# A conditioned decoder trunk on one core: sum and copy of each feed-forward unit joined on VectorE, and one recurrent weight group's low part planned 200 positions ahead

## The chip, the cores and the metric

The kernel runs on one core of a Trainium2 chip. Five engines of that core work side by side, each through its own list of instructions in a fixed order: TensorE (PE in the profile; PEld is its weight load), VectorE (DVE), ScalarE (ACT), GpSimd (POOL) and SyncE (SP), which starts nearly all DMA transfers. They wait for each other by semaphores. An instruction that has to wait holds up everything behind it on its own engine.

The metric is the device time of one execution in microseconds. Before the change it is 1255.91 us, the median of three executions (1254.83 to 1256.75).

## The reference

One inference step of a two-layer decoder for a prompt (1 sequence of 512 tokens) and a batch of samples (8 sequences of 8 tokens), with D_MODEL 1024 and a feed-forward width D_FF of 2816, all in float32:

```python
for l in range(DEPTH):                                   # DEPTH = 2
    sh1, sc1, g1, sh2, sc2, g2 = ada_mod(c, ada_w[l], ada_b[l], 6)
    h = modulate(rms_norm(x, norm_g[l, 0]), sh1, sc1)
    if l < N_A_LAYERS:                                   # layer 0
        out, nbuf, h_last = recurrent_block(h, ...)
    else:                                                # layer 1
        q = apply_partial_rope(...(h @ attn_w_q[j])..., pos)
        out = sliding_sink_attention(q, k_all, v_all, sinks, p0) @ attn_w_o[j]
    x = x + g1[:, None, :] * out
    h = modulate(rms_norm(x, norm_g[l, 1]), sh2, sc2)
    x = x + g2[:, None, :] * swiglu(h, ffn_w_in[l], ffn_w_out[l])

def recurrent_block(h, ...):
    xr, yg = jnp.split(h @ w_in, 2, axis=-1)
    xr, new_buf = causal_dwconv(xr, conv_buf, conv_w, conv_b)
    o, h_last = rg_lru(xr, gate_w, gate_b, lam, h0)      # h = a*h + u, step by step
    return (o * jax.nn.gelu(yg, approximate=True)) @ w_out, new_buf, h_last

def swiglu(h, w_in, w_out):
    gate, up = jnp.split(h @ w_in, 2, axis=-1)
    return (jax.nn.silu(gate) * up) @ w_out
```

`ada_mod` is silu(c) times a weight matrix of 1024 x 6144, for each layer. Between the layers one key/value projection is made.

## The kernel before

**Tokens and precision.** The 576 tokens are kept as two halves h=0 and h=1 of 288 columns (256 of the prompt, 32 of samples). Activations lie as 128 channels by 288 columns. Every float32 operand of a product is split into a high part (rounded to the type that TensorE reads) and a low part (what is left); a product of one 128x128 weight block with one activation block is three matmuls: high weight by high activation, high weight by low activation, low weight by high activation.

**Weights.** They come by DMA in groups ("units") into four raw tiles. For each unit ScalarE casts the high part (tile names `wh`) and VectorE then subtracts it from the raw tile for the low part (also `wh`); this is `convert()` (L1036). The raw tile is free for the next DMA once the low part is made. Units 0 to 17 belong to the recurrent layer's input and gate weights; unit 18 is the first group of the recurrent output weight, whose tiles are raw25, wh49 (high) and wh50 (low). The conditioning weights (`ada_w`) come into five tiles `reg`; from each of them TensorE makes short matmuls with a stationary block `cz` (shown as `ada<-reg,cz`).

**Recurrent layer.** For each channel block VectorE, GpSimd and ScalarE make the gates, the products and a scan along the columns (`TENSOR_TENSOR_SCAN` in the profile); the scan's result, multiplied by the gelu of the other branch (tiles `ta69` to `ta72`), is split into a high and a low part (tiles `sl`; sl79 and sl80 are such a pair). `mm89` is the first block of the output projection: 24 matmuls over eight channel blocks, with wh49 and wh50 as weights, the first five of which are scanned well before.

**Feed-forward.** There are 22 units of 128 hidden channels per layer. For all but the first three, `seven()` (L1383) makes the two inner products (gate and up) for both token halves by a seven-product scheme of 2x2 blocks in place of eight: products "11", "12", "S1", "S2", "S3", "22", "S4" of 12 matmuls each. "S2", "S3" and "22" accumulate in one PSUM tile, bank "b": after S2, VectorE adds a copy of product "11" (`p1`, a `ta` tile) in place, then copies the sum out to `u2` (a `td` tile); S3 accumulates on the same tile and so its first matmul waits for both the sum and the copy. S4 goes to another bank, "e". This happens in 38 units, 19 for each layer. In the profile the sum reads `TENSOR_TENSOR mm<-mm,ta` and the copy `COPY td<-mm`; the matmuls of S2 use `h`, `tb`, `ta` and `sl` tiles by the unit, and those of S3 begin with `tb`.

**What sets the order.** The program is written once in a plain order and recorded: every instruction becomes an `Op` (L133 to L227) with a priority, its place in that order plus a bias. `schedule()` (L229) then plays the five engines through a table of estimated durations; on each engine it takes, among the ops that are ready or will be soon, by priority and time, and gives out the PSUM banks and buffers as they come free. The order that it finds is what each engine runs. `early(n)` (L578) lowers the priority number of what is written in it by n, so that it is planned as if it stood n positions further ahead. `together()` (L148) makes one `Op` of several instructions, which then stand directly behind each other. `HALVES` (L41) holds, by unit number, into how many pieces a low part is cut and how many positions ahead its cast and its low part are planned; units that are not in it have (1, 0). Since the planner goes by sums of durations, a change at one place can alter its choices at others.

All instructions are issued by one line, L491, so the profile's groups have to be told apart by tiles and operations.

Of the kernel before, what the change touches and what calls it, by code (L numbers as in the profile page):

```python
# [16 lines left out]
ALU = mybir.AluOpType  # L17
# [10 lines left out]
HC = 288  # L28
# [9 lines left out]
SWW = 2500.0  # L38
BETA = 0.75
ST = (1, 1, 1)  # L40
HALVES = {101: (2, 0), 103: (2, 60), 108: (1, 60)}  # L41
EW = EP = EA = EK = E1 = ER = 0
EN = 30
ES = 150
# [473 lines left out]
def trunk_kernel(ctx, tc, a):  # L518
    nc = tc.nc
    rec = Recorder(a["shadow"])  # L520
    V, S, G, T, Q = (Engine(rec, n, o) for n, o in (("DVE", nc.vector), ("ACT", nc.scalar), ("POOL", nc.gpsimd), ("PE", nc.tensor), ("SP", nc.sync)))
# [10 lines left out]
    def ps(pool=pmm, tag="mm"):  # L532
        cnt[0] += 1
        return rec.tile(pool, tag, NMM if tag == "mm" else (8 - NMM), RMM if tag == "mm" else 1, [P, 512], F32, f"{tag}{cnt[0]}")
# [12 lines left out]
    td = Slots(rec, cp, "td", SLOT, NTD)  # L547
# [29 lines left out]
    @contextmanager  # L577
    def early(n):  # L578

        rec.bias -= n  # L580
        yield
        rec.bias += n
# [453 lines left out]
    def convert():  # L1036
# [4 lines left out]
        u.hi, u.lo = whs(), whs()  # L1041
        parts, ahead_ = HALVES.get(nconv[0], (1, EW))
        with early(ahead_):
# [57 lines left out]
    def residual(h, o, c, g, last):  # L1101
        xp, xs = x[h][:, c, 0:HP], v48(x[h][:, c, HP:HC])
        V.scalar_tensor_tensor(xp, o[:, 0:HP], mp(g, c), xp, ALU.mult, ALU.add)
        t = ta()
        V.tensor_tensor(v48(t.f[:, 0:32]), v48(o[:, HP:HC]), msam(g, c, h), ALU.mult)
        (V if c >= KC - 2 else G).tensor_tensor(xs, xs, v48(t.f[:, 0:32]), ALU.add)
        t.done()
        if last and (g != L1 + G2 or c < KC - 1):
            square(h, c)
# [148 lines left out]
    for m in range(KC):  # L1258
# [3 lines left out]
            lambda h, o, m=m: residual(h, o, m, G1, True),  # L1262
# [8 lines left out]
    def ffn(l, g, after):  # L1271
# [95 lines left out]
        def pump(want=lambda: True):  # L1367
            while todo and (whs.live + todo[0][0] <= 2 * NHI):
                todo.popleft()[1]()
            assert want()  # L1370
            load_more()

        def right(name):

            if name in ("T2", "T3", "T4"):
                return [(p.r[:, 0:HC], q.r[:, 0:HC]) for p, q in X2[int(name[1])]]
            h, c0 = {"B11": (0, 0), "B21": (0, 4), "T1": (1, 0), "B22": (1, 4)}[name]
            v = h4r(h)
            return [(v[:, k, 0, :], v[:, k, 1, :]) for k in range(c0, c0 + 4)]
# [3 lines left out]
        def seven(i, name):  # L1383

            pump(lambda: (i, name) in W)
            w = W.pop((i, name))
            bank, ops = {"11": ("a", "B11"), "12": ("a", "B21"), "S1": ("e", "T1"), "S2": ("b", "T2"), "S3": ("b", "T3"),
                         "22": ("b", "T4"), "S4": ("e", "B22")}[name]
            b = B.setdefault(i, {})
            if bank not in b:  # L1390
                b[bank] = ps()
            o = b[bank][:, 0:HC]
            first = name in ("11", "S1", "S2")
            for k, (xh, xl) in enumerate(right(ops)):
                hi, lo = [w.r[:, q + k * P : q + (k + 1) * P] for q in (0, H2)]
                T.matmul(o, hi, xh, start=first and k == 0, stop=False, skip_group_check=True)
                T.matmul(o, hi, xl, start=False, stop=False, skip_group_check=True)
                T.matmul(o, lo, xh, start=False, stop=k == 3, skip_group_check=True)
            w.done()
            pump()  # L1400
            if name == "11":
                b["p1"] = ta()
                S.copy(b["p1"].f[:, 0:HC], o)
            elif name == "S1":
                b["p5"] = td()
                S.copy(b["p5"].f[:, 0:HC], o)
            elif name == "S2":

                V.tensor_tensor(o, o, b["p1"].f[:, 0:HC], ALU.add)
                b["p1"].done()  # L1410
                b["u2"] = td()
                V.tensor_copy(b["u2"].f[:, 0:HC], o)
            elif name == "12":

                b["g"] = ta()
                S.activation(b["g"].f[:, 0:HC], o, AF.Silu)
            elif name == "S3":

                y = b["p5"].f[:, 0:HC]
                V.tensor_tensor(y, o, y, ALU.add)  # L1420
            elif name == "22":

                y = b["g"].f[:, 0:HC]
                V.tensor_tensor(y, y, o, ALU.mult)
                whole(0, i, b["g"])
                del B[i]
            else:

                y, z = b["u2"].f[:, 0:HC], b["p5"].f[:, 0:HC]
                V.tensor_tensor(y, o, y, ALU.add)  # L1430
                S.activation(y, y, AF.Silu)
                G.tensor_tensor(z, y, z, ALU.mult)
                b["u2"].done()
                whole(1, i, b["p5"])

        def whole(h, f, t):
            m = mid[h][f] = (sl(F32R), sl(F32R))
            split(m[0].r[:, 0:HC], m[1].r[:, 0:HC], t.f[:, 0:HC])
            t.done()
# [20 lines left out]
        def emit():  # L1460
# [4 lines left out]
            for k in range(len(GROUPS)):  # L1465
                if k == 1 and l == 0:
                    sink_setup()
                for i in range(max(PLAIN, n_), n_ + GROUPS[k]):

                    if i == PLAIN:  # L1470
                        for j, w in ((0, "11"), (1, "11"), (0, "12")):
                            seven(i + j, w)
                    seven(i, "S1")
                    seven(i, "S2")
                    if i == PLAIN:
                        seven(i + 1, "12")
                    elif i > PLAIN + 1:
                        seven(i, "12")
                    if i > PLAIN and i + 1 < n_ + GROUPS[k]:
                        seven(i + 1, "11")  # L1480
                    seven(i, "S3")
                    ada_pace(2)
                    seven(i, "S4")
                    seven(i, "22")
# [628 lines left out]
```

## Time and profile before

| | before |
|---|---|
| time, median of three (us) | 1255.91 (1254.83 to 1256.75) |
| profiled execution: time (us) | 1255.3 |
| profiled execution: span (us) | 1253.5 |
| PE busy | 1240.7 us, 99% |
| DVE busy | 897.9 us, 72% |
| ACT busy | 658.8 us, 53% |
| POOL busy | 480.3 us, 38% |
| granted TensorE clock | 0.998 |

The profile shows one execution. In a timeline each row gives the start in microseconds, how long the group of equal instructions behind it ran, the engine, the operation with its output and inputs by tile (numbers left out), the shape, the count, and in square brackets how long the engine was idle just before and what it waited for. Neighbouring matmuls overlap: the duration of a group runs to the end of its last one, and the next group starts before that end, so the pace is read from the difference of two starts, not from the durations. A row in which the wait is a DMA ends with the tile that had to land. The table of stretches gives the busy time of each engine in a window, then the clock, the share of the DMA engines' time that was used, and GB/s.

### The profile page before, as it was taken

Reading aid. Unit: us, or ns where it says so; the run is one execution under the profiler, and the core shown is the slowest. Engines: PE = TensorE matmul, PEld = TensorE weight load, DVE = VectorE, ACT = ScalarE, POOL = GpSimd, SP = SyncE. Lnnn points to the kernel's source line nnn. Section 1 sums busy time; section 2 is a strip of 40 time slices with the busy share of each in tenths; the row PEclk is TensorE's granted clock in tenths of the full one; section 3 lists DMA queues with packets and bytes.
Section 4 is the critical chain, followed back from the end, with each engine's and each line's share of the span. In section 5 each row is a group of like instructions: output and inputs, shape, how many; then the busy total and the mean of one; then the engine's idle time right before and its main releaser. Section 6 shows DMA issues by size and latency. Waiting matters only on the chain.

```text
span 1253.5 us, 25617 instructions
## 1 busy us (share of the span) xinstructions
PE 1240.7 (99%) x9675; PEld 1179.6 (94%) x9675; DVE 897.9 (72%) x2194; ACT 658.8 (53%) x1474; POOL 480.3 (38%) x671
## 2 busy tenths in 40 slices
PE   8999999999999999999999999999999999999997
PEld 7888999999998999999999998999999999999997
DVE  7989784786675677567568878558767658757856
ACT  4798963753342354245358679548425425514533
POOL 3478550122451454345124536100435346335510
PEclk9999999999999999999999999999999999999999
DMA  9966454417455645446423420422332323323222
GB/s 317 296 207 220 155 168 154 156 47 224 152 179 167 205 120 186 156 166 186 117 68 67 93 60 28 124 85 98 91 98 82 101 85 101 100 78 93 81 89 76
DMA packets 221838, 165.42 MB, mean 132 GB/s; under 512 B 23725, under 2 KB 206985, under 8 KB 221682
## 3 DMA queue, kind: packets, MB, share of 16 engines
q1 hardware_dynamic: 221266, 163.45, 42.7%
q8 instruction: 76, 1.25, 0.4%
q14 instruction: 48, 0.39, 0.1%
q0 software_dynamic: 448, 0.32, 0.1%
HBM read 160.85 MB, written 4.87 MB: 132 GB/s over the span
## 4 chain that ended last, share of the span: by engine, by line
PE 93%; ACT 3%; DVE 3%; issue 1%; POOL 0%; DMA 0%; DVEq 0%; ACTq 0%; SPq 0%; POOLq 0%
PE mm L491 88%; PE ada L491 5%; ACT sl L491 1%; DVE sl L491 1%; ACT ta L491 0%; DVE wh L491 0%; DVE ta L491 0%; ACT L491 0%; DMA raw<-in_ffn_w_out_dram 0%; ACT tb L491 0%; ACT wh L491 0%; DVE tb L491 0%; DVE x L491 0%; DVE h L491 0%; DVE mm L491 0%
## 5 line engine op out<-in xcount | busy, mean ns | idle before, releaser
L491 PE MATMUL mm<-h,wh 128*128 128x288 f32 x4128 | 590.3, 297 | 0.5 <-DVE wh L491 0.2
L491 PEld LDWEIGHTS mm<-h,wh 128*128 128x128 f32 x4128 | 559.2, 188 | 11.9 <-issue 6.0
L491 PE MATMUL mm<-sl,wh 128*128 128x288 f32 x3218 | 461.7, 296 | 0.7 <-DVE wh L491 0.5
L491 PEld LDWEIGHTS mm<-sl,wh 128*128 128x128 f32 x3218 | 436.9, 188 | 7.9 <-issue 5.9
L491 ACT CAST wh<-raw 128x512 fp32r<-128x512 f32 (+3 forms) x388 | 269.0, 711 | 299.1 <-PE mm L491 189.1
L491 DVE TENSOR_TENSOR wh<-raw,wh 128x512 fp32r<-128x512 f32 (+4 forms) x390 | 355.3, 931 | 51.5 <-ACT wh L491 46.7
L491 POOL TENSOR_TENSOR raw<-raw 128x512 f32<-128x512 f32 x76 | 111.5, 1466 | 191.5 <-DVE wh L491 135.1
L491 DVE SCALAR_TENSOR_TENSOR x<-mm,mods,x 128x256 f32<-128x256 f32 x160 | 77.3, 483 | 126.1 <-PE mm L491 125.5
L491 POOL TENSOR_TENSOR x<-x,ta 128x32 f32<-128x32 f32 x120 | 41.7, 347 | 242.9 <-DVE ta L491 242.8
L491 POOL TENSOR_TENSOR raw<-raw,raw 128x512 f32<-128x512 f32 x76 | 113.7, 1496 | 4.2
L491 PE MATMUL mm<-tb,wh 128*128 128x288 f32 (+1 forms) x488 | 88.9, 296 | 1.4 <-DVE td L491 1.4
L491 POOL TENSOR_TENSOR td<-td,td 128x288 f32<-128x288 f32 x38 | 31.2, 820 | 131.2 <-ACT td L491 131.2
L491 PEld LDWEIGHTS mm<-tb,wh 128*128 128x128 f32 x488 | 72.8, 188 | 2.8 <-DVE td L491 1.9
L491 ACT ACTIVATE ta<-x 128x288 f32<-128x288 f32 (+1 forms) x56 | 24.6, 443 | 61.8 <-POOL x L491 39.2
L491 PE MATMUL mm<-ta,wh 128*128 128x288 f32 (+1 forms) x254 | 56.1, 297 | 0.0
L491 DVE TENSOR_TENSOR td<-mm,td 128x288 f32<-128x288 f32 x76 | 33.6, 452 | 23.9 <-PE mm L491 23.6
L491 PE MATMUL ada<-reg,cz 128*32 128x512 f32 (+1 forms) x408 | 47.2, 547 | 0.0
L491 PEld LDWEIGHTS mm<-ta,wh 128*128 128x128 f32 x254 | 41.7, 188 | 1.7 <-ACT sl L491 0.8
L491 ACT COPY td<-mm 128x256 f32<-128x256 f32 (+1 forms) x102 | 33.5, 354 | 14.4 <-PE mm L491 13.4
L491 DVE TENSOR_TENSOR sl<-td,sl 128x288 fp32r<-128x288 f32 x50 | 32.8, 655 | 5.9 <-ACT sl L491 5.6
L491 ACT COPY ta<-mm 128x288 f32<-128x288 f32 (+1 forms) x50 | 18.7, 377 | 34.6 <-PE mm L491 33.4
L491 DVE TENSOR_TENSOR mm<-mm,ta 128x288 f32<-128x288 f32 x38 | 17.7, 466 | 26.8 <-PE mm L491 26.8
(215 smaller groups left out, 1313.5 us busy)
## 6 DMA issues: line engine op xcount, KB each, us to landing
raw<-in_ffn_w_in_dram SPq DMA_DIRECT2D x88, 512.0 KB
reg<-in_ada_w_dram SPq DMA_DIRECT2D x72, 512.0 KB
raw<-in_ffn_w_out_dram SPq DMA_DIRECT2D x32, 384.0 KB
raw<-in_ffn_w_out_dram SPq DMA_DIRECT2D x32, 320.0 KB
raw<-in_rnn_w_in_dram SPq DMA_DIRECT2D x16, 512.0 KB
reg<-in_kv_ada_w_dram SPq DMA_DIRECT2D x14, 512.0 KB
wh<-in_ada_w_dram SPq DMA_DIRECT2D x24, 256.0 KB
raw<-in_rnn_w_out_dram SPq DMA_DIRECT2D x8, 512.0 KB
```

The costliest lines, as they stand in the source:

```text
L491: self.rec.add(eng, lambda: getattr(obj, name)(*map(real, args), **{k: real(v) for k, v in kw.items()}), cost, outs, ins, func, lat, port, ...
```

## The change

Two edits. The first adds unit 18 to `HALVES` with (1, 200): cast and low part of the first recurrent output weight group are planned 200 positions further ahead. The second takes the tile `u2` before the sum, and makes sum and copy one planned step. No instruction is added or removed on any engine; the orders differ.

```diff
@@ -38,7 +38,7 @@
-HALVES = {101: (2, 0), 103: (2, 60), 108: (1, 60)}
+HALVES = {101: (2, 0), 103: (2, 60), 108: (1, 60), 18: (1, 200)}
@@ -1406,10 +1406,11 @@
             elif name == "S2":
 
-                V.tensor_tensor(o, o, b["p1"].f[:, 0:HC], ALU.add)
+                b["u2"] = td()
+                with rec.together():
+                    V.tensor_tensor(o, o, b["p1"].f[:, 0:HC], ALU.add)
+                    V.tensor_copy(b["u2"].f[:, 0:HC], o)
                 b["p1"].done()
-                b["u2"] = td()
-                V.tensor_copy(b["u2"].f[:, 0:HC], o)
```

On PE 99 of some 9100 instructions stand elsewhere, on DVE 95, ACT 48, POOL 14 and SP 5. Three places show the kinds.

The first is VectorE at the unit of the first layer whose bank is mm166 (its copy of "11" is ta162, its `u2` is td36); wh145, wh147 and wh149 are low parts of feed-forward output weights. Before:

```order
L491 TENSOR_TENSOR wh145_5348<-raw68_5284,wh144_5340 128x640
L491 TENSOR_TENSOR mm166_5331<-mm166_5331,ta162_5256 128x288
L491 TENSOR_TENSOR wh147_5363<-raw69_5292,wh146_5350 128x640
L491 COPY td36_5371<-mm166_5331 128x288
L491 TENSOR_TENSOR td35_5336<-mm166_5331,td35_5336 128x288
L491 TENSOR_TENSOR wh149_5401<-raw70_5328,wh148_5381 128x640
```

After:

```order
L491 TENSOR_TENSOR wh145_5344<-raw68_5270,wh144_5326 128x640
L491 TENSOR_TENSOR mm166_5329<-mm166_5329,ta162_5253 128x288
L491 COPY td36_5357<-mm166_5329 128x288
L491 TENSOR_TENSOR wh147_5368<-raw69_5301,wh146_5360 128x640
L491 TENSOR_TENSOR td35_5340<-mm166_5329,td35_5340 128x288
L491 TENSOR_TENSOR wh149_5397<-raw70_5334,wh148_5383 128x640
```

The copy stands directly behind its sum, and the low part wh147 behind both. On TensorE at the same unit (mm164 is product "11" of the next unit, mm165 the bank of this unit's S1 and S4; the matmuls with tb59 begin S3), before:

```order
L491 MATMUL mm166_5331<-sl122_3841,wh138_5238 128x288
L491 MATMUL mm166_5331<-sl123_3862,wh138_5238 128x288
L491 MATMUL mm166_5331<-sl122_3841,wh138_5238 128x288
L491 MATMUL mm164_5230<-h02_3363,wh139_5215 128x288 x12
L491 MATMUL mm165_5307<-h12_3629,wh141_5274 128x288 x4
L491 MATMUL mm166_5331<-tb59_3707,wh140_5246 128x288
L491 MATMUL mm166_5331<-tb60_3718,wh140_5246 128x288
```

After:

```order
L491 MATMUL mm166_5329<-sl122_3841,wh138_5262 128x288
L491 MATMUL mm166_5329<-sl123_3862,wh138_5262 128x288
L491 MATMUL mm166_5329<-sl122_3841,wh138_5262 128x288
L491 MATMUL mm164_5232<-h02_3363,wh139_5172 128x288 x12
L491 MATMUL mm166_5329<-tb59_3707,wh140_5243 128x288
L491 MATMUL mm166_5329<-tb60_3718,wh140_5243 128x288
```

Four matmuls of S4 that stood between S2 and S3 now stand behind S3. Sum and copy are neighbours on VectorE in 28 of the 38 units before as well; in ten there are one to three instructions between them. Ahead of this place, wh140 (the low part with which raw65 is used up, so that raw68 can be loaded) stood on VectorE behind the sums, the copy td34, wh137, sl149, wh139, wh138 and td33 of its neighbourhood; it now stands directly behind wh137, ahead of td33 and wh138, with wh139 and sl149 moved ahead of the copy. The second place is VectorE in the recurrent layer; wh50 is the low part of unit 18, and sl66, sl62 and sl69 are results of scans. Before:

```order
L491 SCALAR_TENSOR_TENSOR ta66_2343<-ta66_2343,sl44_1899 128x300
L491 TENSOR_TENSOR sl72_2441<-sl72_2441,tb52_2378 128x300
L491 TENSOR_TENSOR ta66_2343<-ta66_2343,sl70_2431 128x300
L491 SCALAR_TENSOR_TENSOR ta68_2372<-ta68_2372,sl57_2139 128x300
L491 TENSOR_TENSOR wh50_2545<-raw25_2013,wh49_2448 128x1024
L491 SCALAR_TENSOR_TENSOR sl66_2321<-sl67_2422,hA_80,ta64_2311 128x300
L491 SCALAR_TENSOR_TENSOR sl69_2365<-sl70_2431,ta66_2343 128x300
```

After:

```order
L491 SCALAR_TENSOR_TENSOR tb46_2251<-sl62_2278,sl63_2413 128x300
L491 SCALAR_TENSOR_TENSOR tb48_2292<-sl66_2321,sl67_2422 128x300
L491 TENSOR_TENSOR sl63_2413<-sl63_2413,tb46_2251 128x300
L491 TENSOR_TENSOR wh50_2461<-raw25_2013,wh49_2431 128x1024
L491 TENSOR_TENSOR sl67_2422<-sl67_2422,tb48_2292 128x300
L491 SCALAR_TENSOR_TENSOR ta61_2269<-ta61_2269,sl39_1696 128x300
L491 SCALAR_TENSOR_TENSOR ta64_2311<-ta64_2311,sl47_1825 128x300
```

The low part moves 13 instructions ahead, to directly behind the product sl63 of the recurrence; its cast wh49 moves ahead of two further ACT instructions. The third place is TensorE: a block of short matmuls on the conditioning weights in reg34 to reg37. Before it stands in the middle of a later output block, mm95:

```order
L491 MATMUL mm95_2769<-sl48_2061,wh53_2648 128x288
L491 MATMUL ada70_1998<-reg34_2131,cz_81 32x512 x2
L491 MATMUL ada70_1998<-reg35_2417,cz_81 32x512 x2
L491 MATMUL ada70_1998<-reg36_2427,cz_81 32x512 x2
L491 MATMUL ada70_1998<-reg37_2434,cz_81 32x512 x2
L491 MATMUL mm95_2769<-sl49_2082,wh53_2648 128x288
```

After, it stands directly ahead of the first output block, mm89:

```order
L491 MATMUL mm88_2556<-tb53_2407,wh21_989 128x300
L491 MATMUL ada70_1998<-reg34_2131,cz_81 32x512 x2
L491 MATMUL ada70_1998<-reg35_2417,cz_81 32x512 x2
L491 MATMUL ada70_1998<-reg36_2427,cz_81 32x512 x2
L491 MATMUL ada70_1998<-reg37_2434,cz_81 32x512 x2
L491 MATMUL mm89_2589<-sl20_1396,wh49_2431 128x288
```

It moves 112 matmuls ahead. Behind it, the first matmul on sl79 (`mm89<-sl79,wh49`) also moves: before it stood behind eleven matmuls of mm92, now ahead of them, 23 matmuls behind the start of mm89 instead of 35. Further order changes of the same kind (conversions, loads and copies of neighbouring units exchanged) lie between these places. On SP, three loads into reg tiles now stand ahead of the loads into raw30 and raw31.

## The prediction

> **What bounds the kernel now.** I read the page's totals first, then the chain that ended last, then what TensorE waited for, then the timelines around those waits. The page's span line, its totals and the chain by engine:
>
> ```profile
> span 1253.5 us, 25617 instructions
> PE 1240.7 (99%) x9675; PEld 1179.6 (94%) x9675; DVE 897.9 (72%) x2194; ACT 658.8 (53%) x1474; POOL 480.3 (38%) x671
> PE 93%; ACT 3%; DVE 3%; issue 1%; POOL 0%; DMA 0%; DVEq 0%; ACTq 0%; SPq 0%; POOLq 0%
> ```
>
> TensorE is busy 99% of the span. Its instructions are neither fewer nor shorter after the change, so only its idle time can change. From the table of what TensorE waited for (total us, times, longest):
>
> ```profile
> PE mm L491 <- DVE td L491: 1.4, 2, 0.8
> PE mm L491 <- DVE wh L491: 0.7, 2, 0.5
> ```
>
> The edits aim at these: `td` is a copy of the feed-forward units, `wh` a low part of a weight. How much a wait costs needs the pace without one. Two rows of TensorE's timeline where nothing is waited for:
>
> ```profile
> 169.63 3.33 PE L491 MATMUL mm<-sl,wh 128*128 128x288 f32 x24
> 172.79 2.16 PE L491 MATMUL mm<-h,wh 128*128 128x288 f32 x15
> ```
>
> (172.79 - 169.63) / 24 = 0.132 us for a matmul. The place at which a matmul was due is the start of its predecessors plus 0.132 each; its start less that is the stall, which is more than the idle time in brackets, because the last matmul's overlapping end is not counted idle.
>
> **First term: the feed-forward unit with bank mm166.** TensorE, then VectorE, then ScalarE there:
>
> ```profile
> 381.53 2.29 PE L491 MATMUL mm<-h,wh 128*128 128x288 f32 x16
> 384.60 1.05 PE L491 MATMUL mm<-tb,wh 128*128 128x288 f32 x6 [0.78 <-DVE td L491]
> 385.49 0.96 PE L491 MATMUL mm<-sl,wh 128*128 128x288 f32 x6
> ```
>
> ```profile
> 371.44 1.19 DVE L491 TENSOR_TENSOR wh<-raw,wh 128x512 fp32r<-128x512 f32 x1
> ...
> 375.73 0.68 DVE L491 TENSOR_TENSOR wh<-raw,wh 128x512 fp32r<-128x512 f32 x1
> ...
> 382.26 0.82 DVE L491 TENSOR_TENSOR wh<-raw,wh 128x640 fp32r<-128x640 f32 x1 [1.80 <-ACT wh L491]
> 383.00 0.46 DVE L491 TENSOR_TENSOR mm<-mm,ta 128x288 f32<-128x288 f32 x1
> 383.37 0.81 DVE L491 TENSOR_TENSOR wh<-raw,wh 128x640 fp32r<-128x640 f32 x1
> 384.10 0.45 DVE L491 COPY td<-mm 128x288 f32<-128x288 f32 x1
> ```
>
> ```profile
> 381.50 0.73 ACT L491 CAST wh<-raw 128x640 fp32r<-128x640 f32 x1 [0.91 <-DMA raw<-in_ffn_w_out_dram]
> ```
>
> S3 was due at 381.53 + 16 x 0.132 = 383.64 and began at 384.60: 0.96 lost. The first six then took 385.49 - 384.60 = 0.89 where six take 0.79: 0.10 more, so 1.06 in all. The reader sees two causes. The copy stands behind the low part wh147 (0.73 from start to start). And the sum itself is late: it could begin when S2 is done, about 381.7, but stands behind wh145, which waited 1.80 for a cast that waited 0.91 for a DMA into raw68.
>
> After the change the copy is directly behind the sum: 0.73 sooner. S3 is due sooner too, behind 12 matmuls: 381.53 + 1.58 = 383.11. With the sum still at 383.00 the copy would end at 383.00 + 0.40 + 0.45 = 383.85, a stall of 0.74, and the gain is only 0.96 - 0.74 = 0.22. That all of it goes rests on the sum coming sooner: raw68 can be loaded once wh140 is made, at 375.73 + 0.68 = 376.41 before. wh140 now stands ahead of the sum td33, and of wh138, directly behind wh137, which ended at 371.44 + 1.19 = 372.63; with its own 0.68, and half a microsecond that I allow for its cast, it ends near 373.8. So raw68 is loaded some 2.6 us sooner, its cast no longer waits 0.91, wh145 starts when VectorE came to it before (382.26 - 1.80 = 380.46), and the sum is bound by S2 alone: 381.8, copy to 382.6, 0.5 before S3 is due. I take the whole 1.06 as gone. Ends: 0.22 and 1.06. The four S4 matmuls behind S3 now cover nothing else; wh147 moves 0.4 later, and its users are the output products much later.
>
> **Second term: the unit with bank mm434**, in the second layer. TensorE and VectorE:
>
> ```profile
> 893.89 2.02 PE L491 MATMUL mm<-h,wh 128*128 128x288 f32 x14
> 896.53 1.07 PE L491 MATMUL mm<-tb,wh 128*128 128x288 f32 x6 [0.61 <-DVE td L491]
> 897.44 0.95 PE L491 MATMUL mm<-sl,wh 128*128 128x288 f32 x6
> ```
>
> ```profile
> 894.09 0.47 DVE L491 TENSOR_TENSOR mm<-mm,ta 128x288 f32<-128x288 f32 x1 [1.05 <-PE mm L491]
> 894.47 1.64 DVE L491 TENSOR_TENSOR wh<-raw,wh 128x512 fp32r<-128x512 f32 x1
> 896.03 0.45 DVE L491 COPY td<-mm 128x288 f32<-128x288 f32 x1
> ```
>
> Due at 893.89 + 14 x 0.132 = 895.74, begun at 896.53: 0.79, with the slow start (897.44 - 896.53 - 0.79 = 0.12) 0.91. Here the sum waits for nothing but S2, and only the low part between (894.47 to 896.03) keeps the copy. Joined, the copy runs 894.5 to 894.95, before S3 can be due at 893.89 + 12 x 0.132 = 895.47. The wait goes whole: 0.91. The low part is 0.4 later and ends about 896.5; the two S4 matmuls that it serves come behind S3's twelve, at 897.1 or later. In the other 36 units no wait for the copy shows, so joining is worth nothing there; it costs VectorE perhaps 0.1 per unit (the copy can't start under its sum's tail), in time that it idles.
>
> **Third term: the recurrent layer.** TensorE, ScalarE, VectorE and GpSimd around the first output block:
>
> ```profile
> 160.05 0.43 PE L491 MATMUL mm<-sl,wh 128*128 128x288 f32 x2
> 161.00 2.38 PE L491 MATMUL mm<-sl,wh 128*128 128x288 f32 x16 [0.53 <-DVE wh L491]
> 163.22 0.44 PE L491 MATMUL mm<-ta,wh 128*128 128x300 f32 x2
> ...
> 164.04 1.61 PE L491 MATMUL mm<-h,wh 128*128 128x288 f32 x11
> 165.71 0.40 PE L491 MATMUL mm<-sl,wh 128*128 128x288 f32 x1
> 165.95 1.50 PE L491 MATMUL mm<-h,wh 128*128 128x288 f32 x10
> ...
> 174.79 1.48 PE L491 MATMUL mm<-sl,wh 128*128 128x288 f32 x10
> 176.20 1.92 PE L491 MATMUL ada<-reg,cz 128*32 128x512 f32 x16
> 178.06 8.18 PE L491 MATMUL mm<-sl,wh 128*128 128x288 f32 x59
> ```
>
> ```profile
> 151.89 1.04 ACT L491 CAST wh<-raw 128x1024 fp32r<-128x1024 f32 x1
> ...
> 164.57 1.08 ACT L491 CAST sl<-ta 128x288 fp32r<-128x288 f32 x3
> ```
>
> ```profile
> 159.74 1.21 DVE L491 TENSOR_TENSOR wh<-raw,wh 128x1024 fp32r<-128x1024 f32 x1
> ```
>
> The third matmul was due at 160.05 + 0.26 = 160.31 and began at 161.00 (0.69); the 16 took 163.22 - 161.00 = 2.22 for 2.11 (0.11): 0.80. Its weight wh50 was made from 159.74 to 160.95 although the cast wh49 had ended at 152.93. In its new place it runs about 153.0 to 154.2, six microseconds before it is needed: 0.80 goes.
>
> But what is late next? The first matmul on sl79 waited already: due 164.04 + 11 x 0.132 = 165.49, begun 165.71, the next 0.24 behind it instead of 0.13: 0.22 + 0.11 = 0.33. sl79's cast ends the group at 164.57 + 1.08 = 165.65. After the change TensorE comes to this matmul at 160.05 + 1.95 (the block on reg34 to reg37, 178.06 - 174.79 - 10 x 0.132) + 18 x 0.132 + 5 x 0.137 (those on ta and tb, (164.04 - 163.22) / 6) = 165.06. The block on reg costs its 1.95 in either place, but the eleven matmuls of mm92 that used to stand ahead are gone. If the matmul can start at 165.71 as before, the wait is 0.65 + 0.11 = 0.76. Whether sl79 comes as before is unknown: its scan is the third one, and in VectorE's new order the third channel's product steps stand behind more of the first two's. The nearest price for one more step in its chain is a GpSimd scaling, 0.65:
>
> ```profile
> 153.34 0.65 POOL L491 TENSOR_SCALAR sl<-sl 128x300 f32<-128x300 f32 x1
> ...
> 159.87 1.38 POOL L491 TENSOR_SCALAR sl<-sl 128x300 f32<-128x300 f32 x1
> ```
>
> I take about half, 0.35 (nearer neither end), so a wait of 1.11; the ends are 1.41, and 0 if the low part's leaving the scans brings them forward enough. The term: -0.80 - 0.33 + 1.11 = -0.02, between -1.13 and +0.28.
>
> The second of these rows tells something more: the same scaling took 1.38 while wh50's subtraction ran (159.74 to 160.95), 0.73 more than alone. Moved to 153, the subtraction meets scalings there. The Trainium skill, "SBUF — State Buffer", section "SBUF: two separate sides", says that a VectorE operation with two SBUF inputs and a GpSimd operation that reads SBUF exclude each other for the whole of the instruction that starts first. The row agrees in size; by that rule the sum would end 0.7 us higher than by mine, if GpSimd's chain has no slack to take it.
>
> **The other queues.** The moved block needs reg37, loaded by SP. The table of stretches (PE to POOL busy, clock, DMA share, GB/s):
>
> ```profile
> 151.00:157.00 6.00, 6.00 (x47) 6.00 (x46) 5.63 (x11) 5.97 (x10) 5.21 (x9) 1.00 0.96 339
> 157.00:158.00 1.00, 1.00 (x9) 1.00 (x9) 1.00 (x3) 0.98 (x2) 0.66 (x2) 1.00 0.00 0
> ```
>
> The transfers under way end by 157; the block starts at 160.05: margin 3 us. raw25 is free six microseconds sooner, so SP loads raw29 sooner. The three reg loads that now stand ahead of raw30 and raw31 are held by reg34 to reg37, free at 162 in place of 178. raw30 and raw31 come about 1 us later, for units used long after. Cost 0.
>
> **Sum.** -1.06 - 0.91 - 0.02 = -1.99 on the profiled execution's 1255.3: 1253.3. That execution lay 0.6 below the median of 1255.91, so I predict 1253.9 for the median.
>
> **Rivals.**
>
> *The whole recurrent gain is kept.* For it: wh50 stood directly ahead of the first of the scans, so these may start sooner and sl79 arrive before 165.06. Against: the low part still costs VectorE its 1.21 ahead of these scans, only sooner. -1.06 - 0.91 - 1.13 = -3.10: 1252.8.
>
> *The joining doesn't do what it says in the first layer:* wh145 still holds the sum at 383.00, for another DMA straggler into raw68. Only 0.22 of 1.06 comes: -1.15, 1254.8.
>
> *GpSimd is held up by the moved low part* by 0.73 and passes it on to sl79: -1.26, 1254.7. Against: GpSimd idled 0.40 ahead of a later scaling of the same group, which can take part of it:
>
> ```profile
> 155.01 0.60 POOL L491 TENSOR_SCALAR tb<-tb 128x300 f32<-128x300 f32 x1 [0.40 <-DVE tb L491]
> ```
>
> *Slower: the block on reg stands too early.* If reg37 is not there, TensorE's whole queue stands, where before 112 matmuls lay ahead of it. The reg37 matmuls come at 160.05 + 0.75 x 1.95 = 161.5; all the gain is lost if the load lands 2.0 later, at 163.5, 6.5 us after the transfers of before had ended; slower by over 0.2% needs 166.0. For it: the DMA engines were at 0.96 until 157, and the transfers of that stretch are re-ordered. Against: the margin. With it goes whatever else the altered order hides.
>
> **How the numbers follow.** 0.2%, 2.5 us, is about what a measurement of this kernel can tell from no change: under 1253.4 is faster, over 1258.4 slower. Forecast 0.58; whole recurrent gain 0.18; joining half idle 0.07; GpSimd held up 0.06; late reg or another new stall 0.11. The forecast's 1253.9 lies 0.5 above the line of "faster", with medians that scatter by 1 (runs of 1254.83 to 1256.75), so I give 0.28 of it to faster and 0.30 to same. Faster 0.28 + 0.18 = 0.46, same 0.30 + 0.13 = 0.43, slower 0.11. Range: the whole gain, 1252.8, less 1.2 of scatter, 1251.6, up to no change at the highest run of before, 1256.8.
>
> **What would show it.** Right: no wait of TensorE for `td` in the list; the sum near 381.8 (shifted by what was gained before) with its copy directly behind; wh145's cast without a DMA wait; the low part wh50 at 153; the `ada<-reg` block at 160 without a wait; one wait of about 1 us for sl79 at 165. Wrong: a wait for `reg`, a wait for `td` that stays, the sl79 wait over 1.5 or absent, or new waits for `wh` or `raw` in the feed-forward parts, whose conversions the planner has also shifted.

## The result, and the profile after

The changed kernel takes 1253.69 us, the median of 22 runs (1252.9 to 1256.88), against 1255.76 of 22 runs of the kernel before: 2.07 us less, ratio 0.9986 (95% interval 0.998 to 0.9992). The forecast was 1253.9 in 1251.6 to 1256.8. The profiled execution took 1252.9 with a span of 1251.1, where that of before had 1253.5.

The table of what TensorE waited for, after (total us, times, longest):

```profile
PE mm L491 <- POOL few L575: 1.4, 1, 1.4
PE mm L491 <- ACT raw L491: 1.3, 1, 1.3
PE mm L491 <- ACT sl L491: 1.0, 1, 1.0
PE mm L491 <- POOL few L491: 0.5, 1, 0.5
```

The two rows that the prediction started from are changed: the waits for `td` (1.4 in two) are gone, those for `wh` (0.7 in two) are down to one of 0.2 further down the list, and one of 1.0 for `sl` is new. The other three rows are start-up waits that before has as well.

At bank mm166, TensorE, then VectorE, then ScalarE:

```profile
381.14 1.76 PE L491 MATMUL mm<-h,wh 128*128 128x288 f32 x12
382.73 0.96 PE L491 MATMUL mm<-tb,wh 128*128 128x288 f32 x6
```

```profile
380.02 0.82 DVE L491 TENSOR_TENSOR wh<-raw,wh 128x640 fp32r<-128x640 f32 x1
381.33 0.47 DVE L491 TENSOR_TENSOR mm<-mm,ta 128x288 f32<-128x288 f32 x1 [0.49 <-PE mm L491]
381.84 0.46 DVE L491 COPY td<-mm 128x288 f32<-128x288 f32 x1
```

```profile
379.13 0.72 ACT L491 CAST wh<-raw 128x640 fp32r<-128x640 f32 x1
```

The cast no longer waits for a DMA, the low part wh145 is made from 380.02 to 380.84, the sum waits for S2 alone and the copy ends at 382.30, 0.4 ahead of S3, which starts at the normal pace (382.73 - 381.14 = 1.59 for 12).

At bank mm434, TensorE and VectorE:

```profile
892.19 1.74 PE L491 MATMUL mm<-h,wh 128*128 128x288 f32 x12
893.77 0.95 PE L491 MATMUL mm<-tb,wh 128*128 128x288 f32 x6
```

```profile
892.39 0.47 DVE L491 TENSOR_TENSOR mm<-mm,ta 128x288 f32<-128x288 f32 x1 [1.05 <-PE mm L491]
892.89 0.46 DVE L491 COPY td<-mm 128x288 f32<-128x288 f32 x1
```

No wait there either. In the recurrent layer, TensorE:

```profile
159.45 0.30 PE L491 MATMUL mm<-tb,wh 128*128 128x300 f32 x1
159.68 1.92 PE L491 MATMUL ada<-reg,cz 128*32 128x512 f32 x16
161.53 2.65 PE L491 MATMUL mm<-sl,wh 128*128 128x288 f32 x18
164.01 0.44 PE L491 MATMUL mm<-ta,wh 128*128 128x300 f32 x2
164.29 0.30 PE L491 MATMUL mm<-tb,wh 128*128 128x300 f32 x1
164.43 0.44 PE L491 MATMUL mm<-ta,wh 128*128 128x300 f32 x2
165.87 0.40 PE L491 MATMUL mm<-sl,wh 128*128 128x288 f32 x1 [1.01 <-ACT sl L491]
166.11 0.30 PE L491 MATMUL mm<-tb,wh 128*128 128x300 f32 x1
```

The wait for wh50 is gone and so is any wait for reg37. In their place the matmul on sl79, due at 164.43 + 2 x 0.137 = 164.70, begins at 165.87: 1.17, with the slow start behind it (0.24 for 0.13) 1.28.

To see where the time went without the scatter of whole runs, take for every matmul that stands at the same place in both orders its start in this profile less its start in the first profile of before, and the median of that over a stretch; what it grows or falls from one stretch to the next is what a stage cost or gained. For the changed kernel: -0.46 ahead of the recurrent output, -0.20 behind it; -0.34 ahead of mm166, -1.56 behind it; -1.70 ahead of mm434, -2.61 behind it; -2.34 near the end of the second layer. The first -0.46 has nothing to do with the change (see the last section). So: recurrent layer +0.26, mm166 -1.22, mm434 -0.91, the rest of the second layer +0.27, and -0.28 spread over long stretches without any wait. Another profile of before, against the first, moves by at most 0.05 between these stretches.

### The profile page after: what moved, and what is told of

It is laid out like the page before. It is cut to its first block, busy times and chain, and to the rows that moved or that the text cites. A ratio compares the mean times of both kernels' runs of the same rounds, so it can differ in the third digit from the quotient of the medians.

```text
span 1251.1 us, 25615 instructions
## 1 busy us (share of the span) xinstructions
PE 1239.3 (99%) x9675; PEld 1178.3 (94%) x9675; DVE 898.0 (72%) x2194; ACT 659.4 (53%) x1474; POOL 479.2 (38%) x671
## 4 chain that ended last, share of the span: by engine, by line
PE 94%; ACT 2%; DVE 2%; POOL 1%; issue 1%; DVEq 0%; ACTq 0%; POOLq 0%
PE mm L491 89%; PE ada L491 5%; ACT sl L491 1%; ACT ta L491 0%; DVE sl L491 0%; ACT L491 0%; DVE ta L491 0%; DVE wh L491 0%; ACT tb L491 0%; ACT wh L491 0%; POOL sl L491 0%; DVE x L491 0%; POOL ta L491 0%; DVE h L491 0%; POOL ho L491 0%
## 5 line engine op out<-in xcount | busy, mean ns | idle before, releaser
L491 ACT ACTIVATE td<-td 128x288 f32<-128x288 f32 x38 | 16.8, 443 | 42.1 <-DVE td L491 42.1
```

What stands on the lines that cost most here:

```text
L491: self.rec.add(eng, lambda: getattr(obj, name)(*map(real, args), **{k: real(v) for k, v in kw.items()}), cost, outs, ins, func, lat, port, ...
```

## The experiments

The edits are of order alone. Times are medians of 11 runs, beside 15 to 33 runs of before on the same chip; a ratio is estimated from all these runs and is not the quotient of the two medians.

**Each edit alone.** The second edit without the first:

```diff
-HALVES = {101: (2, 0), 103: (2, 60), 108: (1, 60), 18: (1, 200)}
+HALVES = {101: (2, 0), 103: (2, 60), 108: (1, 60)}
```

> Only the second edit: sum and copy joined, the recurrent weight group planned as before. Every engine's order up to the end of the recurrent layer is then that of the kernel before, and from the feed-forward parts on that of the changed kernel. My theory (the feed-forward waits carry the gain, the recurrent layer comes out even): the two waits for the copy are gone (1.06 and 0.91), the wait for wh50 of 0.53 stays, and the time is 2.0 below before, as with both edits. Rival (the recurrent layer carries a good part of it): less than 1.5 below before, clearly above the kernel with both edits.

Measured: 1254.75 against 1255.31, ratio 0.9997 (0.9988 to 1.0006). By stages: recurrent layer +0.02, mm166 -1.10, mm434 -0.90, but the rest of the second layer +0.81. In the list of waits the two for `td` are gone and that for `wh` stays:

```profile
PE mm L491 <- DVE wh L491: 0.7, 2, 0.6
```

So both feed-forward waits belong to this edit, as expected, and 0.8 is given back in a place that I had costed at nothing. By the whole time the expected 2.0 did not come (0.6): the kernel is less than 1.5 below before, as the rival said, but the recurrent layer, which the rival named as the reason, is at +0.02.

The first edit without the second (the unit's code as before, 18 in the table).

> Only the first edit: unit 18 planned 200 positions ahead, sum and copy as before. The order is the changed kernel's in the recurrent layer and that of before in the feed-forward parts. My theory: the wait for wh50 goes, a wait of about 1.0 for sl79 takes its place and that of the old one of 0.22, and the time is that of before within 0.3. Rival (the new wait has slack elsewhere, so that the 0.8 is kept): 0.8 to 1.1 below before.

Measured: 1255.14 against 1255.31, ratio 0.9997 (0.9988 to 1.0006). By stages: recurrent layer +0.27, mm166 -0.8, mm434 0.00. The recurrent layer loses a little, as with both edits:

```profile
PE mm L491 <- ACT sl L491: 1.0, 1, 1.0
PE mm L491 <- DVE td L491: 0.6, 1, 0.6
```

The one `td` wait of 0.6 is mm434's. The -0.8 at mm166 was not expected: the order there is that of before, and yet S3 was only 0.25 late in this execution:

```profile
382.37 2.30 PE L491 MATMUL mm<-h,wh 128*128 128x288 f32 x16
384.73 1.05 PE L491 MATMUL mm<-tb,wh 128*128 128x288 f32 x6
```

(384.73 - 382.37 - 16 x 0.132 = 0.25.) The load into raw68 explains it: its cast waited only 0.17 here.

```profile
381.62 0.73 ACT L491 CAST wh<-raw 128x640 fp32r<-128x640 f32 x1 [0.17 <-DMA raw<-in_ffn_w_out_dram]
```

In the trace's landing events of that load, 15 of its 16 parts were there by 379.93 in before and the last at 381.47, 1.54 later; here the last came 0.88 behind the others. So the size of the first term depends on one late part of one DMA. The whole time, 0.17 below before, can't tell whether other executions of this kernel have the 0.8.

**The joining at mm166 alone.** In place of the joined code for every unit:

```diff
-                b["u2"] = td()
-                with rec.together():
+                if (l, i) == (0, 9):
+                    b["u2"] = td()
+                    with rec.together():
...
+                else:
+                    V.tensor_tensor(o, o, b["p1"].f[:, 0:HC], ALU.add)
+                    b["p1"].done()
+                    b["u2"] = td()
+                    V.tensor_copy(b["u2"].f[:, 0:HC], o)
```

> Sum and copy joined only in the unit with bank mm166, everything else as before. There the low part wh140, with which raw65 comes free for the next load, keeps its later place on VectorE, while S3 stands behind 12 matmuls as in the changed kernel. My prediction's split of the first term: with the load as late as before, the sum stays behind the low part wh145 at about 1.6 after S2's end, a wait of about 0.74 for the copy stays, and 0.2 of the 1.06 is gained; the time is 0.2 below before. Rival (adjacency of sum and copy alone does it): no wait, 1.0 below before. The wait of the second layer (0.6 in brackets) stays by both.

Measured: 1255.34 against 1255.31; by stages mm166 -0.25, nothing else over 0.1. Sum and copy are neighbours, and yet:

```profile
380.87 0.73 ACT L491 CAST wh<-raw 128x640 fp32r<-128x640 f32 x1 [0.75 <-DMA raw<-in_ffn_w_out_dram]
```

```profile
381.63 0.83 DVE L491 TENSOR_TENSOR wh<-raw,wh 128x640 fp32r<-128x640 f32 x1 [1.64 <-ACT wh L491]
382.38 0.46 DVE L491 TENSOR_TENSOR mm<-mm,ta 128x288 f32<-128x288 f32 x1
382.87 0.46 DVE L491 COPY td<-mm 128x288 f32<-128x288 f32 x1
```

```profile
381.06 1.76 PE L491 MATMUL mm<-h,wh 128*128 128x288 f32 x12
383.38 1.07 PE L491 MATMUL mm<-tb,wh 128*128 128x288 f32 x6 [0.56 <-DVE td L491]
```

S3 is 383.38 - 381.06 - 1.58 = 0.74 late, the wait that the prediction gave for this case. That it agrees to the hundredth is luck: the sum came 1.32 behind the start of the matmuls that follow S2 instead of 1.47, and sum and copy together took 0.95 instead of 0.85. So 0.2 of the first term is the adjacency, as shown here. The rest goes with the earlier load into raw68, in every profile in which the other units are joined too; that the load is earlier because of wh140's earlier place is read from the order, and no run moved wh140 alone.

**Before, once more.**

> The kernel before, a second profile. If the wait at bank mm166 is set by when the load into raw68 lands, and not by the order alone, it differs between executions: between 0.2 and 1.1 by what the kernels with that order have shown (0.96 in the first profile, 0.25 in the kernel with the first edit alone). If the order alone sets it, it is 0.96 again. The wait at mm434, where no load is in the chain, is 0.79 by both.

Measured: 1255.55 in the one run. The wait for the copy at mm166 is as in the first profile: the cast waited 0.94 for the DMA, and TensorE's two waits for `td` are again 1.4 together. So two executions of before have the late part. What it may be late for stands in the traces' DMA packets: besides the loads (queue q1) there is an `instruction` transfer of 16 KB in this stretch. From the table of DMA queues of before, 370 to 382 us (packets, MB, share of the 16 engines' time):

```profile
q8 instruction: 1, 0.02, 0.9%
```

It ran from 377.91 to 379.60, and the late part landed 1.87 behind its end. All fourteen profiles have this transfer. In the four with the order of before at this unit, the load into raw68 was issued only 1.0 to 1.4 ahead of it; the last part came 0.88 to 1.79 behind the other 15, and in each 1.65 to 1.89 behind the end of the transfer. The 0.88 is the kernel with the first edit alone, where the transfer ended 2.57 behind the load's issue and not 2.95 to 3.14 as in the other three. In the ten with this unit and others joined, the load was issued 2.9 to 3.5 ahead of the transfer, which found at most 70 packets of 512 bytes still to start; the last part was at most 0.19 behind, once 0.75. So the late part is hardly chance: that it stands behind the instruction transfer fits all fourteen. It is not shown, since no run moved that transfer and the packets don't name their DMA engine.

**The changed kernel again, and the joining only where it is needed.** The same two branches as above, with another condition:

```diff
-                b["u2"] = td()
-                with rec.together():
+                if l == 0 or i == 3:
...
```

> The changed kernel once more, beside the kernels of this call on their chip. By the first profile: no wait for a copy in the feed-forward parts, a wait of about 1.0 for sl79, and eight starts of the product 22 in the second layer that come 0.08 late each.

> Both edits, but in the second layer sum and copy are joined only in its first unit (bank mm434); the first layer as in the changed kernel. The order is the changed kernel's up to that unit and that of before from there on. My theory (in the second layer's other units the joining only gives 8 x 0.077 = 0.6 back at the starts of product 22): no late starts there, and 0.6 below the changed kernel. Rival (these late starts are hidden elsewhere or stand in before too under another name): the changed kernel's time within 0.2.

Measured, both against 1255.88: the changed kernel 1253.46 (ratio 0.9981, 0.9972 to 0.999), the partly joined one 1253.00 (0.998, 0.9971 to 0.9988). By stages they are alike up to mm434; in the rest of the second layer the changed kernel loses 0.21 and the other gains 0.47. What the joining costs there, on VectorE and TensorE of the changed kernel's first profile:

```profile
966.88 5.02 DVE L491 TENSOR_TENSOR wh<-raw,wh 128x512 fp32r<-128x512 f32 x6
971.81 0.82 DVE L491 TENSOR_TENSOR td<-mm,td 128x288 f32<-128x288 f32 x2
```

```profile
970.22 2.29 PE L491 MATMUL mm<-h,wh 128*128 128x288 f32 x16
972.35 0.64 PE L491 MATMUL mm<-tb,wh 128*128 128x288 f32 x3
972.82 0.29 PE L491 MATMUL mm<-ta,wh 128*128 128x288 f32 x1
```

S3's last matmuls end at 970.4, but the sums that read its bank stand behind six low parts until 971.81, and the first of them ends at 972.26. Product 22, the next on that bank, comes 16 matmuls behind S3 and starts 0.09 behind that end; its three matmuls on `tb` take 0.47 from start to start in place of 0.40. In the partly joined kernel 17 matmuls lie between, as in before:

```profile
970.34 2.43 PE L491 MATMUL mm<-h,wh 128*128 128x288 f32 x17
972.61 0.56 PE L491 MATMUL mm<-tb,wh 128*128 128x288 f32 x3
973.01 0.30 PE L491 MATMUL mm<-ta,wh 128*128 128x288 f32 x1
```

Such a late start comes in eight units of the joined kernels, 0.06 to 0.10 each, 0.68 together in the changed kernel's first profile and 0.61 to 0.64 in the four others that join everywhere; before has one of 0.088. No wait is listed for them, since TensorE is never idle: the delay lies between the first two matmuls. In all eight units of the changed kernel's first profile the read stands behind six low parts, 16 matmuls lie between S3 and product 22, and the read ends 0.06 to 0.09 ahead of it. In before and in the partly joined kernel five of these units have 17 matmuls there, and the other three have 12 with only three low parts ahead of the read; the read ends 0.21 to 0.37 ahead, and no start is late. So that price is shown by stages; in the whole time (0.46 apart, with overlapping intervals) it is only indicated. Not all that differs there is these starts: from 905 us on, the kernel with the second edit alone loses 0.6 more than the changed kernel, in steps of under 0.05 at single matmuls and without any wait, while two executions of the changed kernel differ by 0.03. The cause of that is open.

**The recurrent layer: is there an order that saves the wait?** Four other distances for unit 18. With 150 positions the first matmul on sl79 moves from 23 to 46 matmuls behind the start of mm89:

> Both edits, but unit 18 only 150 positions ahead. The planner then still moves the low part wh50 (two places later on VectorE than in the changed kernel) and the block on reg34 to reg37 ahead, but the first matmul on sl79 stands 46 matmuls behind the start of mm89 instead of 23. My theory (the recurrent gain is lost only because the matmul on sl79 is reached before its cast ends): it is due at about 168, later than the cast, no wait for sl79, and the recurrent layer gains its 0.80 + 0.33 = 1.1; 3.1 below before, 1.0 below the changed kernel. Rival (the recurrence's chain on VectorE bounds the layer, whatever the order on TensorE): another wait of about 1 for one of the later pairs, and the time of the changed kernel.

Measured: 1253.88 against 1255.31, ratio 0.9991 (0.9983 to 1.0). Recurrent layer -0.09, not -1.1. My expectation was wrong: there is no wait for sl79, but another takes its place.

```profile
165.39 1.08 PE L491 MATMUL mm<-h,wh 128*128 128x288 f32 x7
166.86 0.54 PE L491 MATMUL mm<-tb,wh 128*128 128x300 f32 x2 [0.38 <-POOL tb L491]
```

The matmul on tb55, a gate product of a later channel block that GpSimd makes, was due at 166.31 and came at 166.86.

With 260 positions the block on reg and the matmul on sl79 stay where they were in before:

> Both edits, unit 18 planned 260 positions ahead instead of 200. The low part wh50 then stands two places further ahead on VectorE, but the block on reg34 to reg37 stays in the middle of mm95 and the first matmul on sl79 stays 35 matmuls behind the start of mm89, as before. Theory that the recurrence bounds this layer, whatever stands ahead: wh50's wait goes and the wait for sl79 or another pair grows from 0.33 to about 1.0; the layer comes out even within 0.3 and the time is the changed kernel's. Rival (it was the moved block on reg and the earlier place of sl79 that ate the gain): the wait for sl79 stays at 0.33, the layer gains 0.8, and the time is 0.8 below the changed kernel.

Measured: 1254.15 against 1255.88, ratio 0.9991 (0.9982 to 1.0). Recurrent layer +0.06: wh50 is made in time and tb55 comes late again.

```profile
164.84 0.44 PE L491 MATMUL mm<-ta,wh 128*128 128x300 f32 x2
165.74 0.41 PE L491 MATMUL mm<-tb,wh 128*128 128x300 f32 x1 [0.47 <-POOL tb L491]
```

So the block on reg was not what ate the gain. Two more, on the partly joined kernel, and that kernel without the first edit:

```diff
-HALVES = {101: (2, 0), 103: (2, 60), 108: (1, 60), 18: (1, 200)}
+HALVES = {101: (2, 0), 103: (2, 60), 108: (1, 60), 18: (1, 700)}
```

(18: (2, 400) in the next; no entry for 18 in the last.)

> As the kernel with the joining in the first layer and in the unit with bank mm434 only, but unit 18 planned 700 positions ahead. The first output block then begins before the last input block (mm86) has been finished, with the block on reg ahead of it, and the first matmul on sl79 stands 66 matmuls behind its start. Theory that the recurrence's chain bounds this layer: whatever is put ahead, the first matmul that needs its later results waits (for tb55 from GpSimd, or for a pair sl), and the layer comes out even within 0.3 against before. Rival (there is an order in which the wait for wh50 is saved): no wait over 0.2 in it and 0.8 to 1.1 gained.

> As the kernel before this one, but unit 18 planned 400 positions ahead with its low part in two pieces; the block on reg stays where it was in before, and the first matmul on sl79 stands 55 matmuls behind the start of mm89. Theory of the bound by the recurrence: the wait for wh50 is gone, a wait of about 0.5 to 1.0 for tb55 takes its place, even within 0.3. Rival: 0.8 gained.

> As the kernel with the joining in the first layer and in the unit with bank mm434 only, and unit 18 planned as before: the first edit undone. The recurrent layer's order is that of before. My theory (the first edit loses 0.2 in its layer): the recurrent layer as before, with the wait of 0.53 for wh50 back, the feed-forward stages as in the kernel with the first edit, and 0.2 less time than that kernel by the stages. Rival (the first edit is worth something that the stages hide): 0.5 more time.

Measured by stages: recurrent layer +0.78 with 700 positions (waits of 0.6 for `wh`, in the input block that is not yet finished, and of 0.7 for `sl` 25 us later), -0.06 with two pieces at 400 (0.4 for tb55), +0.07 without the edit. Times 1253.80, 1253.99 and 1253.63 against 1255.38, ratios 0.9988, 0.9986 and 0.9987, each with an interval of 0.0009 to both sides; between these three the time tells nothing. Five orders (200, 150, 260, 700, and 400 in two pieces) save the wait for wh50 where it was. Four of them meet another wait of 0.4 to 1.0 within 6 us, for sl79 or tb55, and the recurrent layer ends between -0.1 and +0.3; the fifth, 700, meets one for an input weight first and is worse. That the chain of the recurrence through VectorE, GpSimd and ScalarE bounds this layer, and not wh50, is the reading that fits the four; it is argued and not shown, since a kernel with that chain shortened was not run.

**The two best stages together.** Partly joined, with 150 positions:

> The two orders that came out best by stages put together: sum and copy joined in the first layer and in the unit with bank mm434 only, and unit 18 planned 150 positions ahead. By stages against before: recurrent layer -0.15, first feed-forward layer -1.2, unit mm434 -0.9, the rest of the second layer even; together -2.3 and 0.3 below the same kernel with 200 positions, which the measurement of a few runs may not tell. Rival (the stages do not add up): not below 2.0 under before.

Measured: 1253.07 against 1255.26, ratio 0.9982 (0.9973 to 0.9991); by stages -0.08, -1.19, -0.91 and -0.26, together -2.44, and -2.7 over the whole profile. So the stages keep their worth when put together. The time does not rank the kernels: this one is 2.19 below the before beside it, the partly joined one at 200 positions 2.88, the changed kernel 2.07 and 2.42, and their intervals overlap.

## Why the prediction was right, and where it was not

- **The time** was right: 1253.9 forecast, 1253.69 measured, 2.07 below before where 1.99 was summed. That it came so close is partly luck. By stages the recurrent layer came out 0.28 worse than its term and the rest of the second layer cost 0.27 that was not in the sum; 0.16 more than forecast at mm166 and 0.28 in stretches without any wait offset them.
- **First term, 1.06 at mm166:** right, by its mechanism. 1.22 by stages (1.05 at the matmuls directly behind it). The 0.2 for the adjacency was shown by the joining at mm166 alone; that the rest is the earlier load fits every profile. SyncE issued raw68's load at 374.29, 2.2 sooner than the 376.47 of before; 0.4 of that is this execution's earlier start, so 1.8 where I had 2.6, since wh140 took 1.46 (372.77 to 374.23) and not 0.68. I knew the late part of that load only as a straggler in a rival, and did not see the instruction transfer with which it comes in all four profiles with the old order.
- **Second term, 0.91 at mm434:** right; 0.89 to 0.92 in all ten profiles with this joining, each taken from the matmuls directly ahead of and behind the unit.
- **Third term, -0.02 in the recurrent layer:** the mechanism was right, the size off: +0.19 to +0.27 in the four profiles with this order. The wait for sl79 measured 1.28 with its slow start, where 1.11 was summed; -0.80 - 0.33 + 1.28 makes +0.15, and the last 0.1 lies in small differences that were not traced. The step that was too small is "I take about half, 0.35": sl79's group of casts ended at 165.82, 0.46 added for the earlier start of this execution 166.28, so 0.63 later than the 165.65 of before, close to the end of 0.65. The rows of the chain after, on ScalarE, VectorE and GpSimd:

```profile
164.72 1.10 ACT L491 CAST sl<-ta 128x288 fp32r<-128x288 f32 x3
```

```profile
161.11 0.47 DVE L491 TENSOR_TENSOR sl<-sl,tb 128x300 f32<-128x300 f32 x1 [0.33 <-POOL tb L491]
162.12 1.41 DVE L491 TENSOR_TENSOR_SCAN sl<-sl,ta 128x300 f32<-128x300 f32 x1
```

```profile
158.64 1.85 POOL L491 COPY ho<-sl 128x1 f32<-128x1 f32 x4
160.45 0.62 POOL L491 TENSOR_SCALAR tb<-tb 128x300 f32<-128x300 f32 x1
```

The third scan starts at 162.12 behind a product that waited for a scaling on GpSimd, which stands behind four small copies of 1.85 together. I had priced one step of 0.65 without looking at what GpSimd does ahead of it.

- **"Joining is worth nothing there"** (the other 36 units): wrong. It is the step that failed: I looked only for a wait for the copy, and put the term at nothing. The eight late starts of product 22 cost about 0.6 together, because the orders that the planner finds with the joined step leave 0.06 to 0.09 between the read of S3's bank, behind six low parts, and product 22, where before leaves 0.22 to 0.36. Over the rest of that layer the kernels that join everywhere lost 0.21 to 0.81, the partly joined ones gained 0.01 to 0.47; the late starts are nearly equal in the former (0.61 to 0.68), so the spread within each kind is something else, and open.
- **The rivals.** The whole recurrent gain kept (0.18): did not come in any of the five orders. The joining half idle (0.07): came only when the joining was done at that unit alone. GpSimd held up by the moved low part: the hold-up is there, the loss is not.

```profile
152.08 0.60 POOL L491 TENSOR_SCALAR tb<-tb 128x300 f32<-128x300 f32 x1 [0.40 <-DVE tb L491]
152.65 2.03 POOL L491 TENSOR_SCALAR sl<-sl 128x300 f32<-128x300 f32 x2
155.82 0.75 POOL L491 COPY ta<-shT 128x4 f32<-128x4 f32 x2 [1.15 <-DVE ta L491]
```

wh50 began while the scaling of 152.08 ran, and took 1.45 (152.30 to 153.75) instead of 1.21; the two scalings that met it took 2.03 instead of 1.30, 0.73 more. GpSimd then idled 1.15, so it was not passed on by GpSimd. That agrees with the Trainium skill, "SBUF — State Buffer", section "SBUF: two separate sides": the one of the two that starts first has the ports and the other stands still.
- **The block on reg too early** (0.11 with other stalls): no wait; reg37's load had landed at 157.12 by the landing events, and the block began at 159.68, a margin of 2.6 where 3 was given.

## What to carry to other kernels

A wait that is removed on the bounding engine is worth what the next matmul in the queue lets through: work out when the next dependent instruction's input is ready by its own chain, every queue in it included, before counting the gain. Where a planner reorders, look beyond the waits that the edit aims at: a start that is late by 0.08 shows in no list of waits, and eight of them ate 0.6 us of the 2.1 that the two feed-forward waits were worth. Where a wait ends with a load, look in the DMA packets for what else was under way: here a load issued 1.8 us sooner was nearly through before an instruction transfer began. And join instructions only where a wait shows; a group that must stay together takes freedom from the planner everywhere else.

## What the runs showed of the hardware

The start of a run is not the same length. TensorE's first 32 matmuls, three kernels whose orders are the same up to there (the joining at mm166 alone, before, 260 positions):

```profile
1.44 5.16 PE L491 MATMUL mm<-ident 128*128 128x128 f32 x32 [1.44 <-POOL few L575]
```

```profile
1.43 5.67 PE L491 MATMUL mm<-ident 128*128 128x128 f32 x32 [1.43 <-POOL few L575]
```

```profile
1.44 6.59 PE L491 MATMUL mm<-ident 128*128 128x128 f32 x32 [1.44 <-POOL few L575]
15.44 2.35 PE L491 MATMUL mm<-ident 128*128 128x128 f32 x10
```

They begin at 0.21 us from start to start and change to 0.11 after a time that differs. The traces' records of the granted clock go with it: full clock is granted from 4.45, 5.49 and 7.38 us in these three. The third went slow once more at 15.44 (the same ten take 1.31 in before), and its granted clock is half from 14.20 to 17.61. Ahead of the recurrent layer the profiles differ by up to 3.0 us (from -0.53 to +2.48 against the first of before), more than the whole change brings, and a gain of 2 us shows in single executions only by stages. The differing start fits the Trainium skill, "TensorE: Matmul & The Clock Gate", section 'Part 1: The HAM clock gate (the "warmup" mystery)', by which the window that decides on the clock runs freely and does not begin with the kernel. Over the fourteen profiles of this case the full clock comes between 4.45 and 7.47 us.

A load of 16 parts can be held up by one: 15 parts within 0.8 us and the last 1.54, 1.79, 1.65 and 0.88 later in the four profiles with the old order at mm166, at the same load each time. In the changed kernel, with the load issued 1.8 sooner (2.2 by the clock of the profile), all were there within 0.9. The packets show a 16 KB `instruction` transfer beside the load in the four; it took 1.55 to 1.96 there and 0.94 to 1.29 in the other ten.

A matmul that starts on a wait, or just as its bank comes free, is followed late: at the waits and the late starts treated above the next one came 0.20 to 0.25 behind it instead of 0.13, and where the bank had just come free this was the whole cost.
